# Sixteen sublayers on one core: token-major projections with 512 output columns for 256, and padded 64-row blocks

## The chip, the core and the metric

The kernel runs on one core of a Trainium2 chip. Its engines are named as the profile names them: PE is the matrix engine (a weight load, PEld, puts 128 x 128 values into it, a matmul streams columns past them into a bank of PSUM), ACT and DVE are the two elementwise engines, POOL a third one, SP issues the DMAs. The metric is the device time of one execution in microseconds, lower is better.

## The reference

One sequence of 256 tokens by 1024 channels, in float32, goes through sixteen sublayers in a row. Eight of them are gated feed-forwards, two are plain feed-forwards, six are mixers (convolution, HGRN2, sparse attention, differential attention, pooling, block attention). Each normalises x, projects it, mixes, projects back and adds to x. Cut to what matters here:

```python
def swiglu_ffn(x, w_in, w_out):              # first block, hidden width 2816 = 22 * 128
    gate, up = jnp.split(x @ w_in, 2, axis=-1)
    return (jax.nn.silu(gate) * up) @ w_out
# second block: the same with gate and up apart, hidden width 2752 = 21 * 128 + 64
# third block:  jnp.square(jax.nn.relu(u @ w_ff1)) @ w_ff2, hidden width 4096
q, k, v = ... h @ w_in ...                   # every mixer begins with one projection
y = mix(q, k, v) @ w_out                     # and ends with one
x = x + gain * rmsnorm(y)
```

## The kernel before

**Numbers.** Each float32 operand of a large product is held as a high part and a low part of the type fp32r, and a product takes three matmuls: high by high, high by low, low by high. ACT copies a chunk's high part (`hi`, L283, four instructions) and DVE subtracts for its low part (`lo`, L286, eight instructions).

**Weights.** All weights come as 413 chunks of [128, 2048], 1 MB each, in the order of `_plan`. A chunk "U" is all 1024 input channels (8 blocks of 128) by 256 output columns, a chunk "V" 256 input channels by 1024 output columns. There are 3 raw buffers and 5 pairs of hi and lo. `take` hands out the next chunk.

**Three kinds of product.** In all of them one matmul takes 128 input channels.

- `proj_u` (L516 to L518), channel-major: the weights are loaded into PE, the activations `xh`, `xl` of 256 tokens stream past. 48 matmuls of 256 columns for a chunk.
- `proj_tile` (L528 to L530), token-major: the activations of one tile m of 128 tokens are loaded, the weights stream past. 24 matmuls of 256 columns for a chunk and a tile, 48 for a chunk. They go into half a bank.
- `down` (L549), token-major with a V chunk: the hidden activations (`hh`, `hl`) or a mixer's output (`xh`, `xl` again, the same buffers) are loaded, 512 weight columns stream past. 24 matmuls for a chunk and both tiles. `ks` gives the rows of each block: in the second block's feed-forwards (g00, g01, g10, g11) the last block of hidden channels has only 64 rows, and its twelve matmuls for each sublayer run with 64 rows.

**A sublayer.** `first` (L577) projects four chunks token-major, the first tile of tokens for all four and then the second, into the four banks a0 to a3, so that work can begin when one tile has been normalised. Then come further chunks and the mixing. `finish` (L562) runs the last four V chunks for tile 0 and then for tile 1; while PE does tile 1, ACT and DVE update and normalise tile 0, and PE transposes it (L475), and `split_t` writes it as the next sublayer's `xh`, `xl`. In a gated feed-forward the four chunks' results are gated (ACT L657, DVE L658), and transposed by PE (L659), two chunks a bank.

**Who makes token-major chunks.** `first` in all sixteen sublayers (64 chunks), the memory's keys and values (4 chunks), and after `first` HGRN2 (8), sparse attention (3), differential attention (8) and block attention (6): 93 chunks. Those after `first` lie in PE's queue between the small matmuls of the mixers. They use the two banks "ps" (HGRN2's values the two banks "tr"), one for a chunk.

**Order.** Each engine works through its queue in a fixed order. A scheduler set it when the program was built, from the order of the code and its own estimates, and the code does not say where it put each filler.

Of the kernel before, what the change touches and what calls it, by code (L numbers as in the profile page):

```python
# [21 lines left out]
D = 1024  # L22
# [11 lines left out]
# ---------------------------------------------------------------- host layout  # L34
# A chunk of weights is [128, 2048]: "U" is 8 blocks of 128 input channels by 256
# output columns, "V" is 2 blocks of 128 input channels by 1024 output columns.

def _ffn_plan(tag, nf):
    ng = nf // 2
    out = []  # L40
    for g in range(ng):
        out += [("U", tag, 2 * g), ("U", tag, 2 * g + 1)]
# [5 lines left out]
_U_ORDER = {"diff": (4, 5, 6, 7, 0, 8, 9, 1, 10, 11, 2, 3), "pool": (3, 0, 1, 2), "moba": (2, 3, 0, 1, 5, 6, 8, 9, 4, 7)}  # L48
# [3 lines left out]
def _plan(stages):  # L52
    p = []
    for s in stages:
        if s in ("f00", "f01", "f10", "f11", "g00", "g01", "g10", "g11"):
            p += _ffn_plan(s, 22)
        elif s in ("m0", "m1"):
            p += [("U", s, g) for g in range(4)] + [("V", s, 0), ("V", s, 1)]
            for g in range(4, 16):
                p.append(("U", s, g))  # L60
                if g < 14:
                    p.append(("V", s, g - 2))
            p += [("V", s, g) for g in (12, 13, 14, 15)]
        else:
            n = {"conv": 8, "hgrn": 16, "dsa": 7, "diff": 12, "pool": 4, "moba": 10}[s]
            us = [("U", s, j) for j in _U_ORDER.get(s, range(n))]
            if s in ("pool", "moba"):
                at = 4 if s in ['moba'] else 0
                us[at:at] = [("U", "mem0" if s == "pool" else "mem1", j) for j in range(2)]
            p += us + [("V", s, j) for j in _V_ORDER.get(s, range(4))]  # L70
# [3 lines left out]
def _ucols(w, cols):  # L74
    a = np.zeros((1024, 256), np.float32)
    a[:, :len(cols)] = w[:, cols]
    return a.reshape(8, 128, 256).transpose(1, 0, 2).reshape(128, 2048)


def _chunk(desc, I):  # L80
    kind, s, j = desc
    r = np.arange
    if kind == "V":
# [13 lines left out]
        return w.reshape(2, 128, 1024).transpose(1, 0, 2).reshape(128, 2048)  # L97
    if s[0] == "f":
# [41 lines left out]
    raise ValueError(desc)  # L140
# [50 lines left out]
def _consts():  # L191
    """Constants of the shapes alone."""
# [22 lines left out]
# blocks of channels (and their rows) that make up the pooling groups, two for each  # L215
# [28 lines left out]
# ---------------------------------------------------------------- the program  # L244

class _K:
# [19 lines left out]
    # ---- the stream of weights  # L266
# [23 lines left out]
    def take(self, desc, held=0):  # L290
        """The next chunk's parts; what follows is split as far as there is room beside the chunks held."""
# [26 lines left out]
    def consts(self, act):  # L318
        """What every sublayer needs, and the first one's input."""
# [10 lines left out]
        # causal[t, s] for the second tile of queries; [:, 128:] serves the first  # L330
# [22 lines left out]
    def smalls(self, pool, first, last):  # L353
        """A stretch of the small arrays, on all partitions."""
# [10 lines left out]
    def rsqrt(self, out, ss, inv_n, eps=EPS, pool=None):  # L365
        """out = 1/sqrt(ss * inv_n + eps): a guess from the exponent, then Newton's steps."""
# [18 lines left out]
    def rsqrt_root(self, out, ss, inv_n):  # L385
        """The same by way of a root, with one Newton step."""
# [11 lines left out]
    def prime(self, func, after):  # L398
        """Has the table of an activation function loaded ahead of its use, once a column is there."""
# [8 lines left out]
    def rstd(self, st):  # L408
        """1/sqrt(mean + eps) from the sums of squares of two halves: a root, refined by a Newton step."""
# [35 lines left out]
    def give(self, m, s):  # L445
        """After the last sublayer: a piece of x is returned."""
# [3 lines left out]
    def normed(self, src, pre):  # L450
        """src * gain (given as two halves) with a diagonal matrix of 1/rms(src), and the shift's columns."""
# [39 lines left out]
    def split_2(self, j, o, out):  # L491
        """Two blocks of channels of both tiles of tokens, transposed, as out's hi and lo."""
# [39 lines left out]
    def proj_v(self, w, act, tag="ps"):  # L532
        """Two tiles of 128 tokens by 256 output columns, in one bank."""
# [4 lines left out]

    def down(self, m, acc, w, h, ks, first, last):
        """acc (two banks: the tokens of m by 1024) += h.T @ w over the two blocks of a chunk; ks: rows of each."""  # L540
# [48 lines left out]

    def turned(self, pp):  # L590
        """A chunk of first()'s as proj_u gives it."""
# [9 lines left out]
    def split(self, p, pool):  # L601
        """A bank's hi and lo."""
# [7 lines left out]
    # ---- feed-forward  # L610
    def ffn(self, s, act):
        nc, tc = self.nc, self.tc
        nf = 22
        with tc.tile_pool(name="hp_" + s, bufs=2) as hp:
# [11 lines left out]
            def hidden(f, p):  # L626
# [4 lines left out]
                ragged = s[0] == "g" and f == nf - 1  # L631
                n = 64 if ragged else 128
# [9 lines left out]
            def ks(g):  # L642
                return (128, 64) if s[0] == "g" and g == 10 else (128, 128)

# [4 lines left out]
            p4 = self.first([("U", s, f) for f in range(4)], act)  # L649
# [13 lines left out]
            for g in range(1, 11):  # L663
# [12 lines left out]
            held = [(self.take(("V", s, g), g - 7), hs(g), ks(g)) for g in (7, 8, 9, 10)]  # L676
            return self.finish(acc, held, self.cur_post)

    def mlp(self, s, act):
        nc, tc = self.nc, self.tc  # L680
        with tc.tile_pool(name="hp_" + s, bufs=2) as hp:
# [10 lines left out]
            p4 = self.first([("U", s, g) for g in range(4)], act)  # L692
# [28 lines left out]
    # ---- conformer convolution  # L721
    PE_TAPS = (13,) * 6 + (15, 18)

    def conv(self, act):
        nc, tc = self.nc, self.tc
        with tc.tile_pool(name="cv", bufs=2) as cp:
# [14 lines left out]
            p4 = self.first([("U", "conv", j) for j in range(4)], act)  # L741
            self.rows_ahead("conv")
            # the layer norm's mean and variance are taken about the mean of the first 7 blocks of channels
# [30 lines left out]
            # the variance with tokens on partitions, a tile of them in each bank  # L774
# [27 lines left out]
            # on every partition: the means' 1/D times D / sqrt(var) on a diagonal  # L802
# [25 lines left out]
    # ---- HGRN2: the decay between two tokens is taken apart at the middle of the smallest aligned block  # L828
    # that has them in different halves, into products that are at most 1
# [830 lines left out]
```

## Time and profile before

| what | us |
|---|---|
| runs, median of 3 | 2698.06 (2695.93 to 2703.76) |
| the profiled execution, first to last instruction (span) | 2689.1 |
| median less span: what lies around the program | 9.0 |
| PE busy | 2648.4 (98%) |
| DVE busy | 1992.5 (74%) |
| ACT busy | 1420.0 (53%) |

A busy share of PE is not how close it is to its peak: a matmul's record is longer than the distance to the next one, since they overlap. The distance from start to start is what a matmul costs in a stream. Busy times of groups overlap for the same reason and are not to be added.

### The profile page before, as it was taken

Reading aid. Unit: us, or ns where it says so; the run is one execution under the profiler, and the core shown is the slowest. Engines: PE = TensorE matmul, PEld = TensorE weight load, DVE = VectorE, ACT = ScalarE, POOL = GpSimd, SP = SyncE. Lnnn points to the kernel's source line nnn. Section 1 sums busy time; section 2 is a strip of 40 time slices with the busy share of each in tenths; the row PEclk is TensorE's granted clock in tenths of the full one; section 3 lists DMA queues with packets and bytes.
Section 4 is the critical chain, followed back from the end, with each engine's and each line's share of the span. In section 5 each row is a group of like instructions: output and inputs, shape, how many; then the busy total and the mean of one; then the engine's idle time right before and its main releaser. Section 6 shows DMA issues by size and latency. Waiting matters only on the chain.

```text
span 2689.1 us, 48168 instructions
## 1 busy us (share of the span) xinstructions
PE 2648.4 (98%) x18192; PEld 2426.6 (90%) x18192; DVE 1992.5 (74%) x5892; ACT 1420.0 (53%) x3143; POOL 45.3 (2%) x70
## 2 busy tenths in 40 slices
PE   8999899999999999999999999999999999999999
PEld 8998799999999999998879989989899889998898
DVE  7858896587678875986878678787855876577764
ACT  5455454454554544645655464465744654456543
POOL 0004200000000000000000000000000000000000
PEclk9999899999999999999999999999999999999999
DMA  8743276486434674784448568653555445542452
GB/s 333 287 160 137 90 255 234 164 298 245 160 116 174 259 279 176 289 300 171 158 164 318 214 223 327 226 191 140 183 195 188 168 173 188 188 163 99 175 186 95
DMA packets 91180, 543.94 MB, mean 202 GB/s; under 512 B 10541, under 2 KB 11581, under 8 KB 38082
## 3 DMA queue, kind: packets, MB, share of 16 engines
q1 hardware_dynamic: 90946, 540.85, 55.3%
q8 instruction: 143, 2.34, 0.3%
q14 instruction: 91, 0.75, 0.1%
HBM read 539.69 MB, written 1.13 MB: 201 GB/s over the span
## 4 chain that ended last, share of the span: by engine, by line
PE 85%; DVE 9%; DMA 3%; ACT 2%; issue 1%; SPq 0%; DVEq 0%; ACTq 0%
PE a L549 28%; PE ps L518 12%; PE ps L516 12%; PE ps L517 12%; PE a L528 3%; PE a L530 3%; PE a L529 3%; DVE lo L286 3%; DVE y L768 2%; PE ps L528 1%; PE ps L530 1%; PE ps L529 1%; PE a L1153 1%; DMA raw<-in_wall 1%; PE tr L475 1%; PE a L1196 1%
## 5 line engine op out<-in xcount | busy, mean ns | idle before, releaser
L286 DVE TENSOR_TENSOR lo<-raw,hi 128x256 fp32r<-128x256 f32 x3304 | 1202.9, 417 | 411.2 <-ACT hi L283 408.9
L283 ACT ACTIVATE hi<-raw 128x512 fp32r<-128x512 f32 x1652 | 948.4, 623 | 811.4 <-issue 276.5
L516 PE MATMUL ps<-xh,hi 128*128 128x256 f32 x2784 | 789.5, 284 | 0.0
L518 PE MATMUL ps<-xh,lo 128*128 128x256 f32 x2784 | 789.4, 284 | 0.0
L517 PE MATMUL ps<-xl,hi 128*128 128x256 f32 x2784 | 788.5, 283 | 0.0
L517 PEld LDWEIGHTS ps<-xl,hi 128*128 128x128 f32 x2784 | 533.5, 192 | 3.6
L516 PEld LDWEIGHTS ps<-xh,hi 128*128 128x128 f32 x2784 | 533.4, 192 | 3.5
L518 PEld LDWEIGHTS ps<-xh,lo 128*128 128x128 f32 x2784 | 533.5, 192 | 0.4
L549 PE MATMUL a<-hi,hh 128*128 128x512 f32 x960 | 317.1, 402 | 0.0
L549 PE MATMUL a<-lo,hh 128*128 128x512 f32 x960 | 311.0, 395 | 0.0
L549 PE MATMUL a<-hi,hl 128*128 128x512 f32 x960 | 309.4, 395 | 0.0
L528 PE MATMUL a<-hi,xh 128*128 128x256 f32 x1024 | 291.3, 286 | 4.4 <-ACT xh L483 2.6
L529 PE MATMUL a<-lo,xh 128*128 128x256 f32 x1024 | 289.8, 285 | 0.0
L530 PE MATMUL a<-hi,xl 128*128 128x256 f32 x1024 | 288.0, 285 | 0.5 <-DVE xl L484 0.3
L549 PEld LDWEIGHTS a<-lo,hh 128*128 128x128 f32 x960 | 180.9, 188 | 40.9
L549 PEld LDWEIGHTS a<-hi,hl 128*128 128x128 f32 x960 | 180.3, 188 | 40.7
L549 PEld LDWEIGHTS a<-hi,hh 128*128 128x128 f32 x960 | 175.3, 189 | 44.4 <-issue 10.2
L1018 DVE SCALAR_TENSOR_TENSOR adaj<-adaw,cond 128x1024 bf16<-128x1024 f32 x144 | 175.5, 1219 | 45.6 <-DMA adaw<-in_ada 44.7
L528 PEld LDWEIGHTS a<-hi,xh 128*128 128x128 f32 x1024 | 196.6, 192 | 9.5 <-ACT xh L488 4.8
L530 PEld LDWEIGHTS a<-hi,xl 128*128 128x128 f32 x1024 | 195.1, 192 | 2.0 <-DVE xl L484 1.1
L529 PEld LDWEIGHTS a<-lo,xh 128*128 128x128 f32 x1024 | 196.7, 192 | 0.2
L528 PE MATMUL ps<-hi,xh 128*128 128x256 f32 x336 | 97.3, 290 | 0.0
(364 smaller groups left out, 2961.5 us busy)
## 6 DMA issues: line engine op xcount, KB each, us to landing
raw<-in_wall SPq DMA_DIRECT2D x413, 1024.0 KB, 4.8
adaw<-in_ada SPq DMA_DIRECT2D x144, 512.0 KB, 6.7
G<-in_rows SPq DMA_DIRECT2D x16, 512.0 KB, 5.7
pg<-in_rows SPq DMA_DIRECT2D x12, 512.0 KB, 5.2
xn<-modd SPq DMA_DIRECT2D x12, 512.0 KB, 3.9
cond<-condd SPq DMA_DIRECT2D x7, 512.0 KB
memt<-in_mem SPq DMA_DIRECT2D x4, 512.0 KB
x<-in_x SPq DMA_DIRECT2D x2, 512.0 KB, 5.9
```

The source lines that it names most:

```text
L283: self.nc.scalar.activation(h[:, c], r[:, c], AF.Copy)
L286: self.nc.vector.tensor_tensor(l[:, c], r[:, c], h[:, c].bitcast(F32), op=OP.subtract)
L475: nc.tensor.transpose(o, x, self.ident)
L516: self.nc.tensor.matmul(o, lhsT=wh[:, c], rhs=xh[:, k, :], start=(k == 0), stop=False)
L517: self.nc.tensor.matmul(o, lhsT=wh[:, c], rhs=xl[:, k, :], start=False, stop=False)
L518: self.nc.tensor.matmul(o, lhsT=wl[:, c], rhs=xh[:, k, :], start=False, stop=(k == 7))
L528: self.nc.tensor.matmul(o, lhsT=xh[:, k, t], rhs=wh[:, c], start=(k == 0), stop=False)
L529: self.nc.tensor.matmul(o, lhsT=xh[:, k, t], rhs=wl[:, c], start=False, stop=False)
L530: self.nc.tensor.matmul(o, lhsT=xl[:, k, t], rhs=wh[:, c], start=False, stop=(k == 7))
L549: mm = lambda l, r, i, st, sp: nc.tensor.matmul(acc[i], lhsT=l[:k, t], rhs=r[:k, 1024 * b + 512 * i:1024 * b + 512 * i + 512], start=st, s ...
L768: nc.vector.scalar_tensor_tensor(c, hp[:, j, t:t + S], w(t), c, op0=OP.mult, op1=OP.add)
L1018: self.nc.vector.scalar_tensor_tensor(junk, self.ada_w.pop(n), 1.0, self.cond, op0=OP.mult, op1=OP.mult, accum_out=self.mods[k][:, c:c + 1])
```

## The change

A pair of U chunks becomes a pair of chunks "W": the same two chunks' 512 output columns side by side, the first W with the first 512 input channels, the second with the other 512. `proj_pair` runs them token-major, one tile of tokens at a time: 8 channel blocks, three matmuls each, 512 columns wide, into a whole bank. 24 matmuls take the place of 48. `first` does two pairs for tile 0, then for tile 1. The memory, HGRN2's last eight chunks and the mixers' later chunks go in pairs as well, and the mixers take both chunks of a pair at the same place, so that some chunks are projected earlier than before. One chunk of sparse attention is left as it was. HGRN2's gate is applied in four pieces of 256 columns for a pair instead of two of 512.

In g00 to g11 the 64 missing rows of the last hidden block are set to zero by POOL, in the high and the low part, and `down` runs 128 rows there (the weights had zeros in those rows already).

Of the diff, the core (comments that were taken out, and the tables of order, are left out):

```diff
+def _w(s, a, b):
+    return [("W", s, (a, b), 0), ("W", s, (a, b), 1)]
...
+    if kind == "W":
+        w = np.concatenate([_ublock(s, i, I) for i in j], 1)[512 * desc[3]:512 * desc[3] + 512]
+        return w.reshape(4, 128, 512).transpose(1, 0, 2).reshape(128, 2048)
...
+    def proj_pair(self, ws, act, p, m):
+        xh, xl = act
+        t = slice(128 * m, 128 * m + 128)
+        for k in range(8):
+            wh, wl = ws[k // 4]
+            c = slice(512 * (k % 4), 512 * (k % 4) + 512)
+            self.nc.tensor.matmul(p, lhsT=xh[:, k, t], rhs=wh[:, c], start=(k == 0), stop=False)
+            self.nc.tensor.matmul(p, lhsT=xh[:, k, t], rhs=wl[:, c], start=False, stop=False)
+            self.nc.tensor.matmul(p, lhsT=xl[:, k, t], rhs=wh[:, c], start=False, stop=(k == 7))
...
+    def vpair(self, s, pair, act, tag="ps"):
+        ws = self.take_pair(s, pair)
+        out = []
+        for m in range(2):
+            out.append(self.ps(tag))
+            self.proj_pair(ws, act, out[m], m)
+        return out
...
-    def first(self, descs, act):
-        ws = [self.take(d) for d in descs]
-        out = [[None, None] for _ in ws]
+    def first(self, s, pairs, act):
+        ws = [self.take_pair(s, p) for p in pairs]
+        out = [[None, None] for _ in range(4)]
         for m in range(2):
             for j, w in enumerate(ws):
-                if j % 2 == 0:
-                    p = self.ps(f"a{2 * m + j // 2}")
-                self.proj_tile(w, act, p, m, 256 * (j % 2))
-                out[j][m] = p[:, 256 * (j % 2):256 * (j % 2) + 256]
+                p = self.ps(f"a{2 * m + j}")
+                self.proj_pair(w, act, p, m)
+                for i in range(2):
+                    out[2 * j + i][m] = p[:, 256 * i:256 * i + 256]
...
+                if ragged:
+                    for t in (hh, hl):
+                        nc.gpsimd.memset(t[64:, b].bitcast(F32), 0.0)
...
-                        self.down(m, acc[m], w, hs(g - 1), ks(g - 1), g == 1, False)
+                        self.down(m, acc[m], w, hs(g - 1), (128, 128), g == 1, False)
...
-            ons, qs = [], [heads(3), heads(4)]
-            for j in (5, 6):
-                ons.append(att(qs.pop(0)))
-                qs.append(heads(j))
+            ons, qs = [], [heads(p4[3])]
+            qs += [heads(pp) for pp in self.vprojs("dsa", (4, 5), act)]
+            ons.append(att(qs.pop(0)))
+            qs.append(heads(self.vproj(("U", "dsa", 6), act)))
```

Three places of PE's queue show the order. In the kernel after, `proj_pair` has the lines L567 to L569, `proj_tile` L549 to L551, `proj_u` L537 to L539, `down` L598. First the beginning of the convolution's `first`, tile 0, with buffer numbers: two hi/lo pairs are two chunks. Before, each chunk has eight channel blocks of three matmuls:

```order
L528 MATMUL a0_2521<-hi_2457,xh_2227 128x256
L529 MATMUL a0_2521<-lo_2458,xh_2227 128x256
L530 MATMUL a0_2521<-hi_2457,xl_2228 128x256
...
L528 MATMUL a0_2521<-hi_2473,xh_2227 128x256
L529 MATMUL a0_2521<-lo_2474,xh_2227 128x256
```

After:

```order
L567 MATMUL a0_2425<-hi_2361,xh_2131 128x512
L568 MATMUL a0_2425<-lo_2362,xh_2131 128x512
L569 MATMUL a0_2425<-hi_2361,xl_2132 128x512
...
L567 MATMUL a0_2425<-hi_2377,xh_2131 128x512
L568 MATMUL a0_2425<-lo_2378,xh_2131 128x512
```

The second chunk is reached after 12 matmuls of 512 columns where it was reached after 24 of 256; both fill the bank a0.

The second place is PE's queue just behind the four chunks of a gated feed-forward (f00; `h` is the gated result, `ps` the next channel-major chunk, a0 to a3 the accumulators). Before:

```order
L659 MATMUL tr<-ident,h 128x128 x4
L516 MATMUL ps<-xh,hi 128x256
L517 MATMUL ps<-xl,hi 128x256
L518 MATMUL ps<-xh,lo 128x256
L659 MATMUL tr<-ident,h 128x128
L516 MATMUL ps<-xh,hi 128x256
L659 MATMUL tr<-ident,h 128x128
L549 MATMUL a_504<-hi,hh 128x512
```

After:

```order
L709 MATMUL tr<-ident,h 128x128 x4
L537 MATMUL ps<-xh,hi 128x256
L538 MATMUL ps<-xl,hi 128x256
L539 MATMUL ps<-xh,lo 128x256
...
L537 MATMUL ps<-xh,hi 128x256
L709 MATMUL tr<-ident,h 128x128
L538 MATMUL ps<-xl,hi 128x256
L709 MATMUL tr<-ident,h 128x128
L598 MATMUL a_408<-hi,hh 128x512
```

Between the four transposes and the fifth stand seven matmuls where there were three.

The third place is PE's queue in sparse attention (`e` are the exponentials that are transposed, `kk` by `qT` the scores, `c` by `pT` the values). Before, the sublayer's last chunk lies in small pieces between them:

```order
L1181 MATMUL tr<-ident,e 128x128
L528 MATMUL ps<-hi,xh 128x256
L1181 MATMUL tr<-ident,e 128x128
L529 MATMUL ps<-lo,xh 128x256
L530 MATMUL ps<-hi,xl 128x256
L528 MATMUL ps<-hi,xh 128x256
L1181 MATMUL tr<-ident,e 128x128 x2
```

After, the chunk ends with the two matmuls that stand here, and none of it is left for the three groups of heads that follow:

```order
L550 MATMUL ps<-lo,xh 128x256
L551 MATMUL ps<-hi,xl 128x256
L1232 MATMUL tr<-ident,e 128x128 x2
L1204 MATMUL a_14572<-kk,qT 128x128
L1204 MATMUL a_14573<-kk,qT 128x128
L1204 MATMUL a_14572<-kk,qT 128x256
L1204 MATMUL a_14573<-kk,qT 128x256
L1204 MATMUL a_14591<-kk,qT 128x128
L1247 MATMUL a_14446<-c_14103,pT 128x64 x3
```

Before, 24 matmuls of that chunk stood behind the place that answers to this one, up to the third group of scores.

## Rows read from the trace of the kernel before

**Rows 1.** The page: span, busy time by engine, the chain that ended last.

```profile
span 2689.1 us, 48168 instructions
PE 2648.4 (98%) x18192; PEld 2426.6 (90%) x18192; DVE 1992.5 (74%) x5892; ACT 1420.0 (53%) x3143; POOL 45.3 (2%) x70
...
PE 85%; DVE 9%; DMA 3%; ACT 2%; issue 1%; SPq 0%; DVEq 0%; ACTq 0%
```

**Rows 2.** Token-major groups on PE: line, tiles, xcount | busy, mean ns | idle before.

```profile
L528 PE MATMUL a<-hi,xh 128*128 128x256 f32 x1024 | 291.3, 286 | 4.4 <-ACT xh L483 2.6 <-ACT xh L488 1.5
L529 PE MATMUL a<-lo,xh 128*128 128x256 f32 x1024 | 289.8, 285 | 0.0
L530 PE MATMUL a<-hi,xl 128*128 128x256 f32 x1024 | 288.0, 285 | 0.5 <-DVE xl L484 0.3 <-DVE xl L489 0.2
L528 PE MATMUL ps<-hi,xh 128*128 128x256 f32 x336 | 97.3, 290 | 0.0
...
L528 PE MATMUL tr<-hi,xh 128*128 128x256 f32 x64 | 18.5, 292 | 0.0
L528 PE MATMUL ps<-hi,mh 128*128 128x256 f32 x64 | 18.1, 283 | 0.0
```

**Rows 3.** Timeline of PE in `first` of HGRN2: start, length in us.

```profile
740.86 0.28 PE L528 MATMUL a<-hi,xh 128*128 128x256 f32 x1
740.98 0.28 PE L529 MATMUL a<-lo,xh 128*128 128x256 f32 x1
...
745.06 0.28 PE L530 MATMUL a<-hi,xl 128*128 128x256 f32 x1
```

**Rows 4.** Timeline of PE, convolution's `down`: between two banks, then one bank.

```profile
339.88 0.61 PE L549 MATMUL a<-hi,xh 128*128 128x512 f32 x2
...
342.60 0.61 PE L549 MATMUL a<-hi,xh 128*128 128x512 f32 x2
...
348.72 0.39 PE L549 MATMUL a<-hi,xh 128*128 128x512 f32 x1
348.94 0.39 PE L549 MATMUL a<-lo,xh 128*128 128x512 f32 x1
349.17 0.39 PE L549 MATMUL a<-hi,xl 128*128 128x512 f32 x1
...
349.85 0.39 PE L549 MATMUL a<-hi,xl 128*128 128x512 f32 x1
```

**Rows 5.** Timeline of PE, last `down` of f10, whose blocks have 128 rows.

```profile
733.03 0.39 PE L549 MATMUL a<-hi,hh 128*128 128x512 f32 x1
...
735.11 0.28 PE L528 MATMUL a<-hi,xh 128*128 128x256 f32 x1
```

**Rows 6.** The same place in g10, where 64 rows alternate with 128.

```profile
1773.81 0.40 PE L549 MATMUL a<-hi,hl 128*128 128x512 f32 x1
1774.14 0.49 PE L549 MATMUL a<-hi,hh 64*128 64x512 f32 x1
1774.47 0.39 PE L549 MATMUL a<-lo,hh 64*128 64x512 f32 x1
1774.70 0.39 PE L549 MATMUL a<-hi,hl 64*128 64x512 f32 x1
...
1776.80 0.39 PE L528 MATMUL a<-hi,xh 128*128 128x256 f32 x1
```

**Rows 7.** Transposes behind `first`: what L659 waited for in all, and g01's wait.

```profile
L659 PE MATMUL tr<-ident,h 128*128 128x128 f32 x64 | 13.0, 276 | 1.4 <-DVE h L658 1.4
...
1422.32 0.33 PE L659 MATMUL tr<-ident,h 128*128 128x128 f32 x1 [1.04 <-DVE h L658]
```

**Rows 8.** Windows in sparse attention: us, busy PE, PEld, DVE, ACT, POOL, PEclk, DMA, GB/s.

```profile
1343.00:1353.00 10.00, 9.71 (x54) 6.28 (x52) 6.71 (x32) 7.36 (x26) 0.00 (x0) 1.00 0.29 107
1353.00:1363.00 10.00, 9.27 (x44) 7.83 (x43) 4.81 (x22) 2.88 (x12) 0.00 (x0) 0.63 0.29 105
```

More of the change, by code (lines that the diff above doesn't have):

```diff
@@ L57, in _plan @@
         elif s in ("m0", "m1"):
-            p += [("U", s, g) for g in range(4)] + [("V", s, 0), ("V", s, 1)]
+            p += _w(s, 0, 1) + _w(s, 2, 3) + [("V", s, 0), ("V", s, 1)]
             for g in range(4, 16):
@@ L537, in proj_v, with take_pair, vprojs @@
         return p
+    def proj_pair(self, ws, act, p, m):
[7 more added lines that the diff above has]
+            self.nc.tensor.matmul(p, lhsT=xl[:, k, t], rhs=wh[:, c], start=False, stop=(k == 7))
+    def take_pair(self, s, pair):
+        return [self.take(d) for d in _w(s, *pair)]
+    def vpair(self, s, pair, act, tag="ps"):
[5 more added lines that the diff above has]
+        return out
+    def vprojs(self, s, pair, act):
+        p = self.vpair(s, pair, act)
+        return [[p[m][:, 256 * i:256 * i + 256] for m in range(2)] for i in range(2)]
     def down(self, m, acc, w, h, ks, first, last):
@@ L647, in hs @@
                 return [(hh[:, b], hl[:, b]) for b in range(2)]
-            p4 = self.first([("U", s, f) for f in range(4)], act)
+            p4 = self.first(s, ((0, 1), (2, 3)), act)
             for g in range(2):
@@ L675, in ffn @@
                 self.rows_ahead(s, True)
-            held = [(self.take(("V", s, g), g - 7), hs(g), ks(g)) for g in (7, 8, 9, 10)]
+            held = [(self.take(("V", s, g), g - 7), hs(g), (128, 128)) for g in (7, 8, 9, 10)]
             return self.finish(acc, held, self.cur_post)
@@ L691, in mlp @@
             hs = lambda g: [(groups[g][0][:, b], groups[g][1][:, b]) for b in range(2)]
-            p4 = self.first([("U", s, g) for g in range(4)], act)
+            p4 = self.first(s, ((0, 1), (2, 3)), act)
             for g in range(4):
@@ L740, in conv @@
             nc.vector.tensor_tensor(bl, brow, bh.bitcast(F32), op=OP.subtract)
-            p4 = self.first([("U", "conv", j) for j in range(4)], act)
+            p4 = self.first("conv", _U_ORDER["conv"][:2], act)
             self.rows_ahead("conv")
@@ L909, in scores @@
                     nc.vector.tensor_tensor(W[:, :, S - 2 * n:S - n], whole[:, :, :, 0], whole[:, :, :, 1], op=OP.mult)
-            p4 = self.first([("U", "hgrn", j) for j in range(4)], act)
+            p4 = self.first("hgrn", _U_ORDER["hgrn"][:2], act)
             self.rows_ahead("hgrn")
@@ L918, in hgrn @@
                     scores(j, *vals, lev)
-            for j in range(4):
-                pv = self.proj_v(self.take(("U", "hgrn", 8 + j)), act, "tr")
-                nc.scalar.activation(v[:, :, 256 * j:256 * j + 256], pv.rearrange("p (m c) -> p m c", m=2), AF.Copy)
+            for n, s in enumerate(self.HALVES):
+                pv = self.vpair("hgrn", _U_ORDER["hgrn"][6 + n], act, "tr")
+                for m in range(2):
+                    nc.scalar.activation(v[:, m, s], pv[m], AF.Copy)
             es.close()
@@ L1234, in dsa @@
             self.rope2_tables()
-            p4 = self.first([("U", "dsa", j) for j in range(4)], act) + [None] * 3
+            p4 = self.first("dsa", _U_ORDER["dsa"][:2], act)
             self.rows_ahead("dsa")
@@ L1310, in diff @@
             self.rope2_tables()
-            p4 = self.first([("U", "diff", j) for j in _U_ORDER["diff"][:4]], act)
+            p4 = self.first("diff", _U_ORDER["diff"][:2], act)
             self.rows_ahead("diff")
@@ L1326, in diff @@
             masks = [self.causal[:, 128:], self.causal]
-            chunk = lambda j: self.vproj(("U", "diff", j), act)
+            chunks = lambda i: self.vprojs("diff", _U_ORDER["diff"][i], act)
             def heads(pp, name):
@@ L1475, in pool @@
         with tc.tile_pool(name="po", bufs=2) as pp:
-            p4 = self.first([("U", "pool", j) for j in (3, 0, 1, 2)], act)
+            p4 = self.first("pool", _U_ORDER["pool"], act)
             self.rows_ahead("pool")
@@ L1527, in moba @@
         nc, tc = self.nc, self.tc
-        p4 = self.first([("U", "moba", j) for j in _U_ORDER["moba"][:4]], act)
+        p4 = self.first("moba", _U_ORDER["moba"][:2], act)
         self.rows_ahead("moba")
@@ L1539, in moba @@
             masks = [self.causal[:, 128:], self.causal]
-            chunk = lambda j: self.vproj(("U", "moba", j), act)
+            chunks = lambda i: self.vprojs("moba", _U_ORDER["moba"][i], act)
             def key(pp):
```

87 lines of the change are left out of this document (46 added, 41 removed).

## Prediction

> **What bounds the kernel now.** I read the page first. PE is busy for 2648.4 of 2689.1 us, and 85% of the chain that ended last is PE, DVE 9%, DMA 3% [rows 1]. So the kernel is a stream of matmuls with 41 us of holes in it, 8 of them before the first one, and what a matmul costs is the distance to the next one's start. The groups of the token-major matmuls say how many there are and what they wait for [rows 2], the timelines give the distances [rows 3 to 6], and waits and windows say where PE is held up or runs thinly [rows 7, 8].
>
> Rows 2 also say what they do not wait for. Before L529, the only one of the three that reads `lo`, PE sat idle for 0.0 us, and what L528 and L530 waited for was `xh` and `xl`, the activations. The stream of weights is ahead of PE at these places, so a faster PE does get faster.
>
> **The change part by part.**
>
> *Wider matmuls.* L528 occurs 1024 + 336 + 64 + 64 = 1488 times [rows 2], once for each channel block and tile, which is 93 chunks of 16. One chunk stays, so 92 chunks of 48 matmuls, 4416 of 256 columns, become 2208 of 512. In `first`, 35 starts lie 4.20 us apart from the first to the last, 0.120 us each [rows 3], so two cost 0.240 us. The 512-column price has two rows. In the convolution's `down`, twelve matmuls from 339.88 to 342.60 take 2.72 us, 0.227 us each, and in its last chunk, where the order is high by high, low, high into a single bank, five steps from 348.72 to 349.85 take 1.13 us, 0.226 us [rows 4]. In a feed-forward's `down` nine steps take 2.08 us, 0.231 us [rows 5]. The first is the nearer row: it loads `xh` and `xl` from the same two buffers as `proj_pair`, streams the same `hi` and `lo`, and its last chunk has the very order of `proj_pair`. I take 0.227. The gain is 2208 x (0.240 - 0.227) = 28.7 us; at the 0.231 us of [rows 5] it is 19.9 us. Read as a rule, each matmul carries some 0.013 us beside its columns, whatever its width, and half of them go away. 64 of the 92 chunks lie in `first`, where PE runs without a break, so 20.0 of the 28.7 us are on the path at once; the other 28 chunks lie in mixers, where PE is the filler of longer chains, and part of their 8.7 us could be lost there. I charge that below.
>
> The Trainium skill has a rule that speaks against this gain (TensorE: Matmul & The Clock Gate, section Back-to-back issue gap): at full clock the gap is the columns over 2.4 GHz plus 2.5 ns, which would be 109 ns for 256 columns and 216 ns for 512. By that rule a pair saves 2.6 ns and all of them 5.7 us. The rows show 120 and 227 ns, so the share beside the columns is five times as large here, and I go by the rows.
>
> *Padded rows.* In g10's last chunk ten matmuls from 1773.81 to 1776.80 take 2.99 us [rows 6], where nine of f10 take 2.08 us [rows 5] and ten would take 2.31. The 0.68 us more come at the changes between 64 and 128 rows: into a change a step is 0.33 instead of 0.23, out of it 0.33 again, and between two matmuls of 64 rows it is 0.23, as with 128. There are two tiles in each of four sublayers, and the same rows stand there, so padding saves 8 x 0.68 = 5.4 us. The zeros cost eight instructions on POOL, which is busy for 45 us in all [rows 1]; they are issued when a buffer comes free, two chunks ahead of the use, and hide behind some 10 us of PE. If POOL were late, the last chunk would wait for it, at most about a microsecond each time.
>
> *The entry of a sublayer.* PE waits 4.4 us before L528 and 0.5 before L530, of which 1.5 + 0.2 us are for blocks that come one at a time (L488, L489) [rows 2]. A block was asked for every 0.36 us and is now asked for every 0.68, and the blocks 4 to 7 after 12 wide matmuls. I count 1.0 us of gain, at least 0 and at most 2.
>
> *Later results.* The first chunk's columns were complete for both tiles after 5 of 8 parts of `first`, 14.3 of 22.9 us, and are now after 3 of 4, 16.4 of 21.8 us. The third's and the fourth's now come together at the end. Who needs them at once are the ten feed-forwards: PE transposes the gated results behind `first`. The one long wait there was 1.04 us in g01, 1.4 us in all [rows 7]. The order puts seven matmuls for three in front of the fifth transpose, 0.5 us more of cover, against a third chunk that is 2.9 us nearer to the end. Bounds: below by the loss of the old waits, 1.4 us of gain; above by g01's 1.04 us in each of ten, 10.4 us. I take 3 us, near the lower end, since most of the sublayers show no such wait now.
>
> *Filler used earlier.* In sparse attention 24 matmuls of 256 columns, 2.9 us, that lay between the small ones of the later heads now come before them. That stretch is the thinnest of the kernel: from 1353 to 1363 us PE has 44 matmuls, and the granted clock is 0.63, so part of it runs at 1.2 GHz instead of 2.4 [rows 8]. Bounds: 0, if the chain of softmaxes sets the end in either order; 2.9 us of holes and as much again if a further 6 us run at the lower clock, 6 us. I take 2, nearer to 0 because the filler is moved and not removed. For differential and block attention and HGRN2, whose pairs are bunched in the same way, I take 1 us together (0 to 6).
>
> *The sum.* 28.7 + 5.4 + 1.0 - 3 - 2 - 1 = 29.1 us less in the span: 2689.1 becomes 2660.0. The median stands 9.0 us above the span, so 2698.06 becomes 2669.0. DMA moves the same bytes, and ACT and DVE split the same chunks. DVE, at 74%, is the next in line, but not in this step.
>
> **The rivals.** A measurement of this kernel can tell about 0.3%, 8.1 us, from no change.
>
> *The price of the feed-forward rows.* The wide matmuls run at 0.231 us as in [rows 5]. Then the gain is 19.9 + 5.4 + 1.0 - 6 = 20 us, 2678. For it: that row is a product of weights in the same buffers, too. Against it: the loaded buffers, by which the rows differ, are those of [rows 4].
>
> *Width is worth nothing.* If the columns alone set the distance, a wide matmul takes 0.240 us, and what is left is 5.4 + 1.0 - 6, about 0: 2698. Against it stand all of [rows 4, 5], which no 512-column row at 0.240 contradicts. The skill's rule above, taken at its 5.7 us, ends near this rival, at 2692.
>
> *The late results cost more.* The gating behind `first` takes the full 1.04 us in ten places and the mixers take their upper bounds: 10.4 + 12 in place of 6. The gain falls to 13 us, 2685, or below 8 us together with the 0.231.
>
> *Slower: PE thins out and the clock falls.* The mixers' later chunks keep PE dense between small matmuls. If bunching them leaves stretches like that of 0.63 in sparse attention [rows 8] also in differential and block attention and pooling, PE runs them at half its clock. Ten us at 0.63 hold about 7.4 us at half clock, which do some 3.7 us of full-clock work and so lose as much. The change is slower when the loss passes the 35 us of the first three parts, that is at some 70 us more at 1.2 GHz. For it: the only such stretch in a mixer with filler is just where that had run out. Against it: the later chunks of the other mixers stay spread over them, and 70 us is most of two mixers.
>
> *That the change doesn't do what it says* is out: the order shows the wide matmuls and the padded rows.
>
> **How the numbers follow.** The forecast, 0.227 us and about the losses that I took, has 0.62. The price 0.231 has 0.17, late results 0.09, width worth nothing 0.05, slower 0.03; for 0.04 the losses do not come at all and a stretch of half clock goes with them, which gives 2657. Faster by over 0.3% are the forecast, the price 0.231, most of the late results and the last: 0.89. Within 0.3%: 0.07, the rest of the late results and most of the width; slower: 0.04. The range for 8 in 10 runs from 2658, with 28.7 + 6 + 2 us and the old waits gone, a little over 38 us, to 2684, with 0.231 us or the larger losses, but not both.
>
> **What would show it.** Starts of `proj_pair` 0.227 us apart, in `first` and elsewhere; `first` in 21.8 us instead of 22.9; no step of 0.33 at the end of g00 to g11; idle time before the transposes of the gated results near 4 us rather than 1.4; 41 us of holes in PE growing to some 45; a granted clock no lower than before in the mixers. I am wrong if the wide matmuls' distance is not that of the convolution's `down`, or if PE's holes grow by over 10 us.

## The result, and the profile after

The changed kernel takes 2675.5 us (median of 4 runs, 2675.0 to 2677.0) where the kernel before takes 2697.3 (4 runs, 2695.9 to 2703.8): a ratio of 0.9921, with a 95% interval of 0.9907 to 0.9935. The forecast was 2669.0, with a range of 2658 to 2684. The spans of the two profiled executions, on which the sum was made, are 15.5 us apart, 2689.1 and 2673.6, where the sum had 29.1.

The page of the changed kernel, first the span, the engines and the chain, then its costliest token-major groups and what the transposes waited for (columns as in [rows 1, 2]), and the loads of ScalarE's function tables:

```profile
span 2673.6 us, 43797 instructions
...
PE 2621.3 (98%) x15984; PEld 2307.9 (86%) x15984; DVE 1993.4 (75%) x5892; ACT 1442.2 (54%) x3161; POOL 47.9 (2%) x78
...
PE 85%; DVE 11%; ACT 3%; DMA 1%; issue 1%; SPq 0%; ACTq 0%; DVEq 0%
```

```profile
L567 PE MATMUL a<-hi,xh 128*128 128x512 f32 x512 | 203.2, 399 | 2.7 <-ACT xh L504 2.5
L568 PE MATMUL a<-lo,xh 128*128 128x512 f32 x512 | 201.9, 395 | 0.0
...
L496 PE MATMUL tr<-ident,xn 128*128 128x128 f32 x300 | 46.9, 281 | 22.5 <-DVE xn L481 13.7 <-DVE ident L350 8.2
...
L709 PE MATMUL tr<-ident,h 128*128 128x128 f32 x64 | 13.6, 276 | 1.5 <-DVE h L708 1.5
...
L707 ACT ACT_TABLE_LOAD x16 | 20.5, 1283 | 0.3
L435 ACT ACT_TABLE_LOAD x10 | 12.8, 1283 | 0.2
```

In PE's timeline stand `first` of f11 and the end of g10, the place of [rows 6]:

```profile
889.22 0.39 PE L567 MATMUL a<-hi,xh 128*128 128x512 f32 x1
...
891.72 0.39 PE L569 MATMUL a<-hi,xl 128*128 128x512 f32 x1
...
1756.24 0.40 PE L598 MATMUL a<-hi,hl 128*128 128x512 f32 x1
...
1758.57 0.40 PE L567 MATMUL a<-hi,xh 128*128 128x512 f32 x1
```

Eleven steps from one wide matmul's start to the next take 2.50 us, 0.227 us each, the price taken. Ten steps at the end of g10 take 2.33 us where [rows 6] had 2.99: the steps of 0.33 are gone. The gated transposes wait 1.5 us in all, as before (1.4 in [rows 7]), so what the forecast feared there did not come. But the transposes of `xn` wait 13.7 us for VectorE, where they waited 4.3 before. ScalarE has 22 us more work, of which 18 are fourteen more table loads: L707's group was nine and L435's three. The same three groups in the kernel before:

```profile
L475 PE MATMUL tr<-ident,xn 128*128 128x128 f32 x300 | 46.3, 280 | 13.1 <-DVE ident L329 8.4 <-DVE xn L460 4.3
L657 ACT ACT_TABLE_LOAD x9 | 11.5, 1283 | 0.6 <-PE a L530 0.5
L414 ACT ACT_TABLE_LOAD x3 | 3.8, 1283 | 0.1
```

PE's holes, the span less its busy time, grew from 40.7 to 52.3 us. That is 11.6 us more, and the prediction had named a growth by over 10 us as a sign that it is wrong.

Where it went by stretches, from the first matmul of one `first` to that of the next; the second column is 0.62 us for each of the 46 pairs, with the padding and the entries where they belong (35.1 us in all, before the 6 us of losses that the forecast charged):

| stretch | pairs | expected gain, us | found, us | kernel e7 below, us |
|---|---|---|---|---|
| f00, conv | 4 | 2.5 | 2.2 | 2.5 |
| the other seven feed-forwards | 15 | 15.8 | 5.5 | 20.7 |
| HGRN2 | 6 | 3.7 | 6.1 | 6.2 |
| sparse attention | 3 | 1.9 | 9.5 | 10.4 |
| differential attention | 6 | 3.7 | 0.0 | -0.3 |
| pooling to m1, block attention among them | 12 | 7.5 | -7.7 | 3.6 |

Four rows are far off: the feed-forwards and block attention lost much more than was charged, differential attention gave nothing of its 3.7 us, and sparse attention gained. HGRN2 gave 2.4 us more than the price; PE's waits there fell from 2.0 to 0.4 us.

### The profile page after: what moved, and what is told of

It is laid out like the page before. It is cut to its first block, busy times and chain, and to the rows that moved or that the text cites. A ratio compares the mean times of both kernels' runs of the same rounds, so it can differ in the third digit from the quotient of the medians.

```text
span 2673.6 us, 43797 instructions
## 1 busy us (share of the span) xinstructions
PE 2621.3 (98%) x15984; PEld 2307.9 (86%) x15984; DVE 1993.4 (75%) x5892; ACT 1442.2 (54%) x3161; POOL 47.9 (2%) x78
## 4 chain that ended last, share of the span: by engine, by line
PE 85%; DVE 11%; ACT 3%; DMA 1%; issue 1%; SPq 0%; ACTq 0%; DVEq 0%
PE a L598 27%; PE ps L539 12%; PE ps L537 12%; PE ps L538 12%; DVE lo L307 4%; PE a L567 3%; PE a L568 3%; PE a L569 3%; DVE y L818 2%; PE a L1204 1%; PE tr L496 1%; PE ps L567 1%; PE ps L568 1%; PE ps L569 1%; PE a L1247 1%
## 5 line engine op out<-in xcount | busy, mean ns | idle before, releaser
L537 PE MATMUL ps<-xh,hi 128*128 128x256 f32 x2784 | 790.1, 284 | 0.0
L539 PE MATMUL ps<-xh,lo 128*128 128x256 f32 x2784 | 788.2, 283 | 0.0
L537 PEld LDWEIGHTS ps<-xh,hi 128*128 128x128 f32 x2784 | 533.2, 192 | 3.4
L539 PEld LDWEIGHTS ps<-xh,lo 128*128 128x128 f32 x2784 | 533.4, 192 | 0.4
L598 PE MATMUL a<-hi,hh 128*128 128x512 f32 x960 | 315.3, 399 | 0.0
L598 PE MATMUL a<-lo,hh 128*128 128x512 f32 x960 | 311.5, 395 | 0.0
L598 PE MATMUL a<-hi,hl 128*128 128x512 f32 x960 | 309.7, 395 | 0.0
L598 PEld LDWEIGHTS a<-lo,hh 128*128 128x128 f32 x960 | 180.9, 189 | 41.8
L598 PEld LDWEIGHTS a<-hi,hl 128*128 128x128 f32 x960 | 180.6, 188 | 40.8 <-DVE hl L656 0.2
L598 PEld LDWEIGHTS a<-hi,hh 128*128 128x128 f32 x960 | 175.6, 189 | 35.8 <-ACT hh L655 1.0
L567 PE MATMUL a<-hi,xh 128*128 128x512 f32 x512 | 203.2, 399 | 2.7 <-ACT xh L504 2.5
L568 PE MATMUL a<-lo,xh 128*128 128x512 f32 x512 | 201.9, 395 | 0.0
L569 PE MATMUL a<-hi,xl 128*128 128x512 f32 x512 | 201.0, 396 | 0.0
L567 PEld LDWEIGHTS a<-hi,xh 128*128 128x128 f32 x512 | 97.5, 190 | 26.2 <-ACT xh L504 4.9
L569 PEld LDWEIGHTS a<-hi,xl 128*128 128x128 f32 x512 | 97.5, 190 | 21.7 <-DVE xl L505 1.3
L568 PEld LDWEIGHTS a<-lo,xh 128*128 128x128 f32 x512 | 97.5, 190 | 19.4
L459 DVE TENSOR_TENSOR upd<-a,pg 128x512 f32<-128x512 f32 x48 | 32.8, 687 | 65.8 <-ACT junk L427 65.8
```

The costliest lines, as they stand in the source:

```text
L459: nc.vector.tensor_tensor(t, acc[n], pg[:, s], op=OP.mult)
L537: self.nc.tensor.matmul(o, lhsT=wh[:, c], rhs=xh[:, k, :], start=(k == 0), stop=False)
L539: self.nc.tensor.matmul(o, lhsT=wl[:, c], rhs=xh[:, k, :], start=False, stop=(k == 7))
L567: self.nc.tensor.matmul(p, lhsT=xh[:, k, t], rhs=wh[:, c], start=(k == 0), stop=False)
L568: self.nc.tensor.matmul(p, lhsT=xh[:, k, t], rhs=wl[:, c], start=False, stop=False)
L569: self.nc.tensor.matmul(p, lhsT=xl[:, k, t], rhs=wh[:, c], start=False, stop=(k == 7))
```

## The experiments

**ScalarE's order in the feed-forwards.** In the kernel before, the Silu of the first chunk's gate waited for the whole bank, that is for the 48 narrow matmuls of two chunks; with a pair the bank is complete after 24 wide ones. In f10 the last of them ends 5.6 us after the first matmul of `first`, and ended 5.9 us after it before (548.50 and 549.86 in the traces). So the gate was complete just after the Sqrt in the norm of tile 1 had been issued, and is now complete just before. In f01, f10, f11 and g00 to g11 the scheduler now puts the Silu ahead of that Sqrt. (That it does so because the gate is complete sooner is argued from these times; no run tests it.) ScalarE at f10's entry, first in the kernel before, then changed:

```profile
549.36 0.19 ACT L406 ACTIVATION_READ_ACCUMULATOR junk<-x 128x1 f32 x1
549.59 0.30 ACT L414 ACTIVATE rq<-stx,rb 128x1 f32<-128x1 f32 x1
549.90 1.28 ACT L657 ACT_TABLE_LOAD   x1
...
551.43 1.39 DVE L460 SCALAR_TENSOR_TENSOR xn<-x,ry,G 128x512 f32<-128x512 f32 x2
```

```profile
548.30 0.19 ACT L427 ACTIVATION_READ_ACCUMULATOR junk<-x 128x1 f32 x1
548.50 1.28 ACT L707 ACT_TABLE_LOAD   x1
549.80 0.28 ACT L707 ACTIVATE sg<-a 128x128 f32<-128x128 f32 x1
550.10 1.28 ACT L435 ACT_TABLE_LOAD   x1
551.39 0.29 ACT L435 ACTIVATE rq<-stx,rb 128x1 f32<-128x1 f32 x1
551.70 1.28 ACT L707 ACT_TABLE_LOAD   x1
...
553.80 1.41 DVE L481 SCALAR_TENSOR_TENSOR xn<-x,ry,G 128x512 f32<-128x512 f32 x2
...
554.69 1.29 PE L496 MATMUL tr<-ident,xn 128*128 128x128 f32 x8 [0.75 <-DVE xn L481]
```

From the last sum of squares to `xn` it is 2.07 us before and 5.50 now, and PE's transposes of tile 1 stand behind all 48 matmuls of tile 0 and wait even so. To test it, the Silu was queued behind that Sqrt:

```
                 self.split_t(m, self.normed(self.x[:, m], nxt), act)
+                self.tail = <the Sqrt that normed() just issued>
...
+                        with tc.issue_after(self.tail):
                             nc.scalar.activation(sg[:, m], pp[:, :128], AF.Silu)
```

> The changed kernel, with ScalarE's gate Silu of the first chunks queued behind the Sqrt of the second tile's norm, and nothing else asked for. Theory A (in f01, f10, f11, g00, g01 and g10 the Silu had slipped ahead of that Sqrt, which cost two more table loads and made the second tile's xn some 3.4 us later, so that TensorE waits before its transposes): those waits, 7.8 us in all six, and the 1.2 us before the gated transposes of g10 go away, 8 to 9 us less than the changed kernel, 2667. Rival B (TensorE waits there because it comes through 24 wide matmuls sooner, whatever ScalarE's order): the waits stay within 1 us each and the time within 2 us of 2675.5.

It took 2659.6 us (4 runs, 2655.8 to 2662.2), 15.9 less than the changed kernel. In its trace `xn` starts 2.04 us after the last sum of squares, and the transposes wait for nothing:

```profile
547.58 0.19 ACT L427 ACTIVATION_READ_ACCUMULATOR junk<-x 128x1 f32 x1
547.80 0.29 ACT L435 ACTIVATE rq<-stx,rb 128x1 f32<-128x1 f32 x1
548.11 1.28 ACT L707 ACT_TABLE_LOAD   x1
...
549.62 1.41 DVE L481 SCALAR_TENSOR_TENSOR xn<-x,ry,G 128x512 f32<-128x512 f32 x2
...
550.54 0.61 PE L496 MATMUL tr<-ident,xn 128*128 128x128 f32 x4
```

The seven feed-forwards together went from 1349.0 to 1334.5 us, and the fourteen loads are gone. Theory A holds, and the gain is nearly twice its number. It had counted only the waits that the profile books. In f10 the eight transposes of tile 1 cost PE 1.31 us from start to start, and 0.72 here: in the changed kernel the fifth starts only when the second half of `xn` is done, and the next matmul waits for `xh`. These two pauses of about 0.3 us are hardly booked as idle, because a transpose's record is itself 0.27 us long. In g00 the changed kernel's granted clock was also 0.83 in the ten us from 1090, behind its wait there, and it is 1.00 at that place here.

**Block attention: late keys or spent filler.** The changed kernel's waits there, PE first, then ScalarE:

```profile
2382.72 0.66 PE L1164 MATMUL tr<-ident,memkk 128*128 128x128 f32 x4
...
2393.00 3.15 PE L1164 MATMUL tr<-ident,q 128*128 128x128 f32 x12 [5.03 <-DVE rs_w L402]
...
2455.47 0.73 PE L598 MATMUL a<-hi,xh 128*128 128x512 f32 x2 [2.93 <-ACT xh L1175]
...
2383.42 0.60 ACT L1169 ACTIVATE memk<-tr 128x512 f32<-128x512 f32 x1 [4.41 <-PE tr L1164]
2383.91 0.38 ACT L1186 ACTIVATE q<-a 128x256 f32<-128x256 f32 x1
```

The same transposes of the memory's keys in the kernel before, whose `first` ended at 2390.8:

```profile
2403.54 0.63 PE L1111 MATMUL tr<-ident,memkk 128*128 128x128 f32 x4 [0.20 <-DVE memkk L1420]
```

ScalarE copies the first head's columns out of PSUM (`q<-a`) only behind the memory's keys, in both kernels: the code closes the memory's pool before it opens the heads'. The chain from there to the heads' transposes takes some 10 us. The keys' transposes come 17.8 us after `first` (2364.9 to 2382.7), 12.7 before, and of the 96 wide matmuls that lie ahead of the heads' transposes 20 are left for those 10 us. Two kernels, each undoing one part. e3 projects the memory's keys as a chunk of their own, ahead of the values (code shortened):

```
-    us[at:at] = _w("mem0" if s == "pool" else "mem1", 0, 1)
+    us[at:at] = _w("mem0", 0, 1) if s == "pool" else [("U", "mem1", 0), ("U", "mem1", 1)]
```

> The changed kernel, with the memory's keys and values in block attention as two single chunks again, keys first. Theory A (as a pair the keys are complete 5.1 us later, everything of the block-attention pool starts behind them, and the filler has run out by then): the wait of 5.0 us before the first heads' transposes goes, with most of the 13.7 us at a clock of half speed, for 0.6 us of dearer matmuls: 8 to 10 us less, 2666. Rival B (the later chunks in pairs are what starves that stretch): the wait stays over 3 us, the time within 2 us of 2675.5.

and e4, with the code of before for the later chunks (code shortened):

```
-    "moba": ((2, 3), (0, 1), (5, 6), (8, 9), (4, 7))}
+    "moba": ((2, 3), (0, 1), 5, 6, 8, 9, 4, 7)}
```

> The changed kernel, with the six later chunks of block attention (after first() and the memory) as single chunks at their old places, the memory still as a pair. Theory A (the memory's late keys cause the 5.0 us wait): that wait stays at 4 us or more; only the wait of 2.9 us before out_proj goes, for 1.9 us of dearer matmuls: 0 to 3 us less, 2674. Rival B (bunching the later chunks starves the sublayer): block attention is back at 134 to 136 us instead of 144.6, the time 8 to 10 us less, 2666.

e3 took 2669.6 us (2668.5 to 2671.2), e4 2671.3 (2670.3 to 2673.9): 5.9 and 4.3 us less than the changed kernel. In size both theories A missed: e3 was to gain 8 to 10 us and e4 at most 3. In e3's trace:

```profile
2380.49 0.63 PE L1164 MATMUL tr<-ident,memkk 128*128 128x128 f32 x4 [0.17 <-DVE memkk L1470]
...
2390.97 1.07 PE L1164 MATMUL tr<-ident,q 128*128 128x128 f32 x8
...
2449.85 0.80 PE L598 MATMUL a<-hi,xh 128*128 128x512 f32 x1 [3.84 <-ACT xh L1175]
```

and in e4's:

```profile
2396.79 3.13 PE L1164 MATMUL tr<-ident,q 128*128 128x128 f32 x12 [5.03 <-DVE rs L396]
...
2455.64 0.73 PE L598 MATMUL a<-hi,xh 128*128 128x512 f32 x2 [0.36 <-ACT xh L1175]
```

Each takes away its own wait and leaves the other's. So late keys and spent filler are both real losses: the late keys make the wait of 5 us, the spent filler the one of 2.9 before `out_proj`. Behind each wait PE ran at half clock for a while (behind the second the granted clock is 0.83 from 2450 to 2460). The windows behind the first (columns as in [rows 8]), in the changed kernel and then in e3:

```profile
2385.00:2395.00 10.00, 4.97 (x23) 3.85 (x21) 10.00 (x52) 6.90 (x17) 0.00 (x0) 0.83 0.03 13
2395.00:2405.00 10.00, 9.88 (x34) 5.85 (x34) 8.77 (x44) 8.39 (x26) 0.00 (x0) 0.50 0.01 2
```

```profile
2395.00:2405.00 10.00, 9.81 (x45) 7.16 (x46) 9.65 (x47) 9.14 (x26) 0.00 (x0) 1.00 0.24 99
```

**Do the fixes add, and a better version.** e6 is e2, e3 and e4 in one. e7 is e6 with the memory as a pair again, ahead of `first` (code shortened; its weights move ahead in the plan as well):

```
-        p4 = self.first("moba", ...); self.rows_ahead("moba"); kTm, vm = self.mem_kv()
+        kTm, vm = self.mem_kv(); p4 = self.first("moba", ...); self.rows_ahead("moba")
```

> The kernel of e2_root_first with the memory's chunks of block attention as singles (as in e3_mem_single) and its six later chunks as singles at their old places (as in e4_moba_tail). Theory A (late keys and spent filler are two losses, which add): 5.9 and 4.3 us less than 2659.6, 2649 to 2650, with no wait over 1 us in block attention. Rival B (both took away the same loss, the half-speed stretches): no better than 2653.

> The kernel of e6_three_fixes, but the memory's pair stays a pair and stands ahead of first() instead of behind it. Theory A (what matters is when the memory's keys are there, not the width of their chunk): as e6 or better by the 0.6 us of the pair and the sooner keys, 2646 to 2650. Rival B (without the memory's matmuls behind first() there is too little left to cover the first heads' chain of 10 us): a wait of 3 us or more before the first heads' transposes or scores, 2653 or more.

e6 took 2652.1 us (2650.9 to 2653.9) and e7 2651.0 (2648.1 to 2652.7); their ratios to the kernel before are 0.9826 (0.9807 to 0.9845) and 0.9819 (0.9802 to 0.9836). From e2's 2659.6 e6 gained 7.5 us of the 10.2 that a plain sum gives, between the two theories' numbers; its block attention has no wait over 0.3 us up to the heads' transposes. e7 is 1.1 us better, less than the spread of either, with 0.5 us of wait there. So it counts when the keys are there; whether the pair itself is worth its 0.6 us cannot be told. e7 is the best version found.

**The width alone.** e5 is e2 with each wide matmul as two of 256 columns:

```
-        for k in range(8): ... three matmuls of 512 columns
+        for i, k in [(i, k) for i in (0, 256) for k in range(8)]: ... three of 256, at column i
```

> The kernel of e2_root_first with every wide matmul of the pairs as two of 256 columns (first the left half over all channel blocks, then the right), nothing else changed: layout, stages and ScalarE's order stay. It prices the width alone: 2208 matmuls more. Theory A (0.013 us a matmul beside its columns): 28.7 us more than e2_root_first, 2688. Rival B (the 0.231 us of a feed-forward's down): 19.9 us more, 2679. Rival C (width is worth nothing): 2660. A left half is complete after 24 narrow matmuls of 48, so block attention may lose some of its 5 us wait; that would take 1 to 4 us off each of the three.

It took 2702.8 us (10 runs, 2698.9 to 2709.0), 43 more than e2 and 15 more than theory A's 2688. `first` of g00 in e2 and in e5, where both run up to the transposes without a break:

```profile
1076.34 0.40 PE L567 MATMUL a<-hi,xh 128*128 128x512 f32 x1
...
1086.13 1.03 PE L496 MATMUL tr<-ident,xn 128*128 128x128 f32 x8
```

```profile
1090.81 0.28 PE L567 MATMUL a<-hi,xh 128*128 128x256 f32 x1
...
1100.50 0.60 PE L496 MATMUL tr<-ident,xn 128*128 128x128 f32 x4
```

43 wide ones in 9.79 us are 0.228 each, 80 narrow ones in 9.69 us are 0.121, so a wide one saves 0.0146 here; the token-major matmuls of f10 and f11, without any wait, differ by 1.27 and 1.25 us over 96, 0.013 each. Over 2208 that is 29 to 32 us: theory A's price, and no rival's. The 43 are not all price: summed over the kernel the token-major distances differ by 35 us, PE's waits by 7, and both kernels have stretches at half clock. So the price of the width was not mis-sized; what e5 lost beyond it, over 10 us, lies in part in those waits and was not followed further.

The rule that the prediction set aside (the Trainium skill, TensorE: Matmul & The Clock Gate, section Back-to-back issue gap), 2.5 ns a matmul beside its columns at full clock, is given there for isolated matmuls and would make 5.5 us of these 2208 (the prediction's 5.7 is rounded). No stream of matmuls here has the distance that it gives: 0.109 and 0.216 us by the rule, 0.120 to 0.121 and 0.226 to 0.231 in the rows.

**Sparse attention.** The forecast charged 2 us for the filler that comes earlier. In the trace the sublayer got 9.5 us shorter, and the stretch at the low clock in [rows 8] is gone. e9 undoes the move in e7, e10 makes it alone in the kernel before (code shortened):

```
e9:  -"dsa": ((0, 1), (2, 3), (4, 5), 6)           e10: -qs = [heads(3), heads(4)]
     +"dsa": ((0, 1), (2, 3), 4, 5, 6), ...             +qs = [heads(3), heads(4), heads(5)], then (6)
```

> The kernel of e7_mem_first, with the three later chunks of sparse attention as singles at their old places (first() there stays in pairs). It undoes the earlier use of the filler, and with it one pair, worth 0.6 us. Theory A (the earlier filler is what ended the stretches at the low clock in sparse attention): they come back, 10 to 20 us long, the sublayer takes 112 to 118 us instead of 106.9, the time is 5 to 11 us more, 2656 to 2662, and spreads by more than 8 us over the runs. Rival B (the width did it, since wide matmuls keep TensorE denser): no such stretch, 0.6 us more, 2651.6.

> The kernel before, all matmuls narrow, with one change: in sparse attention the fifth and sixth chunk are projected ahead of the first softmax, as in the changed kernel. Theory A (the place of the filler decides the clock there): no stretch at the low clock in sparse attention, the sublayer takes 110 to 112 us instead of 117 to 123, the time is 6 to 10 us less, 2691, and the runs spread by less than 8 us. Rival B (the width does it): still 117 us or more, within 2 us of the kernel before.

> The kernel before once more, for a second profile: its times spread from 2689 to 2709 on this chip, those of the changed kernel by 2 us. Theory A (the thin stretches of sparse attention run at the low clock for a longer or shorter time): a slower execution differs from the first profile by granted clock in sparse attention and little elsewhere. Rival B (all matmuls or the DMA are slower): the difference is spread over all sublayers.

e9 took 2664.8 us (2662.1 to 2667.2), 13.8 more than e7. Sparse attention took 117.4 us instead of 106.9, and PE's half speed is back. e10 took 2693.6 us (6 runs, 2687.1 to 2694.7), a ratio of 0.9968 (0.9953 to 0.9983); sparse attention took 113.7 us, all at full clock. The windows of the thinnest stretch in e8 (the kernel before once more), e9, e10 and the changed kernel:

```profile
1350.00:1360.00 10.00, 9.21 (x27) 5.24 (x27) 5.87 (x33) 4.76 (x19) 0.00 (x0) 0.51 0.01 2
```

```profile
1336.00:1346.00 10.00, 10.00 (x42) 8.19 (x42) 4.74 (x22) 3.85 (x16) 0.00 (x0) 0.55 0.32 105
```

```profile
1360.00:1370.00 10.00, 9.90 (x67) 7.38 (x67) 6.87 (x34) 6.62 (x25) 0.00 (x0) 1.00 0.01 2
```

```profile
1338.00:1348.00 10.00, 10.00 (x74) 7.81 (x74) 7.24 (x30) 6.06 (x22) 0.00 (x0) 1.00 0.25 96
```

Theory A holds on both sides: the place of the filler decides the clock there, not the width, for e10's matmuls are all narrow. Its numbers held less well. e9 lost more than the 5 to 11 us and spread by 5, not over 8. e10 gained 5.3 us instead of 6 to 10, and its sublayer took 113.7 us and not 110 to 112; f10 and f11 have waits of 1.6 and 1.8 us in its profiled execution that the two profiles of the kernel before do not have. And the place is not the whole gain: at full clock too, e10's sublayer takes 5.9 us more than the changed kernel's 107.8, and e5's, narrow with the filler moved, takes 111.9 where e2's takes 106.8. The price of three pairs is 1.9 us; where the rest of the 5 to 6 us comes from stays open.

e8 gives the kernel before its second profile: 2695.6 us of span, 6.5 more than the first, and 6.0 of them lie in sparse attention, 123.2 us instead of 117.3. The feed-forwards f01 to g00 agree within 0.1 us each.

**Two small ones.** e1 is the kernel before with the padding alone, e11 is e7 with differential attention's later chunks as singles, at the places of before (code shortened):

```
e1:  -return (128, 64) if s[0] == "g" and g == 10 else (128, 128)
     +return (128, 128)                     (and the rows set to zero)
e11: -"diff": ((4, 5), (6, 7), (0, 1), (8, 9), (10, 11), (2, 3))
     +"diff": ((4, 5), (6, 7), 0, 8, 9, 1, 10, 11, 2, 3), ...
```

> The kernel before with the zero padding alone: the last hidden block of g00 to g11 goes through `down` with 128 rows. My theory (each change between 64 and 128 rows costs about 0.1 us in each of its two steps, 0.68 us per tile, eight tiles): 5.4 us less than the kernel before, 2692. Rival (the steps of 0.33 us are covered by something else and padding moves nothing): within 1 us of the kernel before, 2697.

> The kernel of e7_mem_first, with the eight later chunks of differential attention as singles at their old places: four pairs of 48 wide matmuls less, 2.5 us by the price of 0.013. Theory A (bunching these chunks made the waits of 5.8 us there, 3.0 of them at the entry of g11): they fall to 3 us, the time stays within 1 us of 2651. Rival B (the wait at the entry of g11 hangs on where VectorE's queue has the weights' splits, not on the pairs): that wait stays over 2 us, 2653.5.

e1 took 2697.0 us (10 runs, 2686.6 to 2706.5) beside 2701.1 (13 runs, 2688.8 to 2709.0), a ratio of 0.9988 (0.9969 to 1.0008). The time alone does not decide. In its trace the matmuls of `down` in g00 to g11 take 1.4 to 1.6 us less each, 6.0 in all, but the gated transposes of g00 and g10 wait 1.4 and 1.1 us, where they had 0.3 and none. From the first matmul of `first` to that of the next, g01 got 2.0 us shorter and g00, g10 and g11 only 0.3 to 0.4 each, so alone the padding gave little of its 5.4 us in this execution.

e11 took 2652.3 us (2648.6 to 2660.5), e7 2651.0: no difference that can be told. The wait at g11's entry, changed kernel and e11 (e7, from which e11 was made, waits the same 3.01 us there):

```profile
1881.38 1.38 PE L496 MATMUL tr<-ident,xn 128*128 128x128 f32 x8 [3.01 <-DVE xn L481]
```

```profile
1873.37 1.38 PE L496 MATMUL tr<-ident,xn 128*128 128x128 f32 x8 [0.52 <-DVE xn L481]
```

Theory A is right about this wait. The time can't tell it from B: e11's profiled execution is the slowest of its four, 2660.5 us, with a granted clock of 0.50 in the ten us from 1775.5 and from 2407.0, in differential and block attention, where e7's profile has 1.00.

## Why the prediction was right, and where not

*Wider matmuls*, 28.7 us: right in place and size. 0.227 us is what the rows show, and e5 puts the price of the width at 0.013 to 0.0146 us.

*Padded rows*, 5.4 us: right. `down` of g00 to g11 takes 1.3, 1.3, 1.4 and 1.5 us less in the changed kernel, 5.4 in all; no wait of `down` for POOL was seen. That the four sublayers get shorter by as much is not shown by e1, the padding alone.

*Entry*, 1.0 us: PE waits 2.7 us before L567, where [rows 2] had 4.4 and 0.5. The gain is 2.2 us, just past the upper bound of 2.

*Later results*, 3 us: the step that failed. It looked for the loss at the gated transposes, where nothing changed (1.5 us against 1.4). Its sentence that the third and fourth chunk come later overlooked the other side: for tile 0 the bank of the first pair is complete sooner, and on ScalarE its gate went ahead of the norm for tile 1. The prediction let ScalarE's queue stand as it was. That cost 14.5 us in seven feed-forwards (e2). None of the rivals has it. The table's shortfall there is only 10.3 us, because with the order mended these sublayers gain 4.9 us more than forecast (e7's column), mostly in g01 and g11, where PE's waits sum to 2.4 and 2.8 us before and to 0.6 and 0.3 in e7.

*Filler used earlier*, 2 us and 1 us: wrong in sign in sparse attention and too small by far in block and differential attention. In the first the moved filler closed the thin stretch of [rows 8] (e9, e10). In block attention it was the other half of the pair that was missed. The first chunk of a pair is complete only when the second is, and the memory's keys, which a whole chain hangs on, came 5.1 us later (e3); the rest was the filler (e4). Block attention became 10.7 us longer in spite of its cheaper matmuls. In differential attention 3.0 us are the wait at g11's entry (e11). The slower rival named this mechanism, a stretch that thins out and falls to half clock, and gave it the right form in the wrong size; the forecast had looked for a granted clock no lower than before in the mixers, and in block attention it fell to 0.50.

*The offset.* "The median stands 9.0 us above the span" was read as what lies around the program. In every later run the time is 1.8 us above its span, so the profiled execution of before was one of the faster, about 2691 us. Its time in sparse attention varies by 6 us with the clock. So the forecast of 29 was met by 15.5 us in the spans and 21.8 in the medians; 6 of these are the execution.

The sum came out in the range because the two losses, 14 to 15 us in the feed-forwards and some 14 in block attention, were partly paid by 8 us in sparse attention that the forecast did not have. So the price of the matmuls was foreseen, and that the total fell in the range is partly luck: the holes grew by more than the prediction allowed itself. With the two losses mended, e7's span is 42.9 us shorter than that of before.

## To carry to other kernels

When results are made wider, list for each consumer when its operand is complete now: in a pair the first half is later and the second sooner, and a sooner operand can overtake something more urgent in an engine's fixed order. After such a change count the table loads on ScalarE; fourteen more of them were the first sign of 15 us. In a mixer the place of the filler can be worth more than its price, since a thin stretch cost its holes here and then half the clock.

## What was not expected of the hardware

A change of function table costs ScalarE 1.3 us from the load's start to that of the next activation (548.50 to 549.80 above). The Trainium skill (ScalarE: Activation LUTs, section What ACT_TABLE_LOAD costs) gives 1283 ns for the load, which the trace agrees with (1283 in the groups), and a drain of about 1380 ns beside it, which these rows do not show.

Executions of one program differ by how long TensorE runs at half clock: the two profiles of the kernel before have 27 and 48 us at a granted clock of 0.5 in all, e7 has 17. The kernel before spread over 20 us in 13 runs (2688.8 to 2709.0), e7 over 4.7 in 4. e11's slowest execution has such stretches where e7's profile has none.
